# Gate tiles by seven quarter products, with half of the weight sums made by accumulating DMAs

## The chip, the core and the metric

The kernel runs on one core of a Trainium2 chip. TensorE (PE) does matrix products into PSUM, VectorE (DVE) and ScalarE (ACT) do elementwise work, GpSimd (POOL) does little here, and SyncE (SP) issues the DMAs. The metric is the device time of one execution in microseconds. The kernel before takes 1191.26 us (median of 3 runs, 1188.45 to 1191.48).

## The reference, cut to what matters

A decoder of two layers on 512 tokens of width 1024: layer 0 mixes with a gated DeltaNet, layer 1 with sliding-window attention, and after the mixer each layer has a feed-forward part. All is float32. The change lies in the feed-forward part alone:

```python
def swiglu(h, w_gate_up, w_down):
    gu = h @ w_gate_up
    return (jax.nn.silu(gu[..., :D_FF]) * gu[..., D_FF:]) @ w_down
...
    x = x + swiglu(rms_norm(x, ln_ffn[layer]), w_gate_up[layer], w_down[layer])
```

D_FF is 2816, that is 22 tiles of 128 columns for the gate and 22 for the up half.

## The kernel before

Activations lie transposed: 128 features on the partitions, 512 tokens along the free axis, eight such tiles for the width of 1024. A float32 product is made from three matmuls of a rounded type (fp32r): each operand is split into a high half, which is a rounded copy made by ACT (`copy`, line 137), and a low half, which is the rest, made by DVE (`tt`, line 150). `split` (line 165) does both, `weight` (line 179) does it for a weight tile loaded from HBM, into the tags `whi` and `wlo` of the weight pool, with three buffers each. `mm3` (line 190) issues the three matmuls: high x high, high x low, low x high. Every matmul of the profile has line 143.

`ffn` (line 829) works on the 22 pairs of gate and up tiles in two halves of 11. In each half the first gate and up tile are plain projections: 8 blocks of 128 rows times 3 matmuls of 512 columns (`project`, line 198). The other ten tiles go two at a time. Both gate tiles of a pair are plain projections into the banks `pj`, scaled by `rstd` on DVE and put through Silu on ACT (`gate`, line 836). The two up tiles of a pair are made together by `up_pair` (line 934): the two weight tiles and the tokens are seen as a 2 x 2 matrix of quarters (512 of the 1024 rows, one of the two tiles; 256 of the 512 tokens), and their product needs seven products of quarters in place of eight (Strassen in Winograd's form). Each of the seven is 4 x 3 = 12 matmuls of 256 columns. They use three PSUM banks `pa`, `pb`, `pc` of the tag `g`; partial results are held by ACT (`held`, tile `fs`), and products 4, 6 and 7 go on adding into `pa`, so each of them may start only when the value before has been read out of it.

The sums of tokens that the seven products want (`t1` to `t4`) are made once per layer by `token_sums` (line 915), four calls, each with five operations on DVE and one split, into tiles `T`. The sums of weights are made for every pair on DVE (lines 943, 944, 946, 947), in two tiles `ws`, and split. So a pair of up tiles uses four slots of split weights: w0 (the first tile), w1 (two sums), w2 (two sums), w3 (half of the second tile). Two more are used by the gate tiles. `put` (line 846) splits the finished activation. After the 11 tiles of a half the down projection follows: 8 chains of 33 matmuls of 512 columns, in the banks `pj`.

The order of instructions on each engine is not that of the program: a planner in the framework puts them in order, with estimated costs, and gives each tile the buffer that it waits for. What an engine has in its queue is then run strictly in that order. SP's DMA queue likewise: a load waits until its buffer is free, and all later loads wait behind it.

Of the kernel before, what the change touches and what calls it, by code (L numbers as in the profile page):

```python
# [9 lines left out]
F32 = mybir.dt.float32  # L10
F32R = mybir.dt.float32r
# [74 lines left out]
class Builder:  # L86
# [139 lines left out]
    def build(self):  # L226
        tc, nc, a = self.tc, self.nc, self.a
        with ExitStack() as st:
            opened = lambda name, **kw: tc.tile_pool(name=name, bufs=1, reuse_waits="tile", **kw)
            pool = lambda name, **kw: st.enter_context(opened(name, **kw))  # L230
            cp = pool("const")
            self.wpool, self.apool = pool("w"), pool("acta")
            self.dpool = pool("scratch", space=DRAM)
            self.load_constants(cp)
            self.weng = nc.vector
            with opened("layer0", side="right") as self.mpool:
                with self.banks(pj=3, g=2, sc=3):
                    with opened("early", side="right") as ep:
                        self.mem_and_norm(ep)
                        self.gates(ep)  # L240
                    with opened("gdn", side="right") as gp:
                        mix = self.gdn(gp)
                    self.bpool, xp = pool("actb"), pool("x")
                    self.x = [self.t(xp, [P, T], F32, f"x{k}") for k in range(KD)]
                    for k in range(KD):
                        nc.sync.dma_start(self.x[k], a["xT"][:, k, :])
                    self.rstd, self.cosT, self.sinT = (self.t(xp, [P, T], F32, n) for n in ("rstd", "cosT", "sinT"))
                    h = self.output(xp, 0, mix, self.bpool)
            with opened("ffn0", side="right") as fp, self.banks(pj=4, g=4):
                self.ffn(fp, xp, 0, h, self.apool, rope=True)  # L250
            with self.banks(pj=2, g=1, qk=1, pt=2, sc=1):
                with opened("swa", side="right") as sp:
                    mix = self.swa(sp)
                h = self.output(xp, 1, mix, self.apool)
            with opened("ffn1", side="right") as fp, self.banks(pj=4, g=4):
                self.ffn(fp, xp, 1, h, self.bpool)

    def load_constants(self, cp):
# [570 lines left out]
    def ffn(self, fp, xp, layer, h, apool, rope=False):  # L829
# [3 lines left out]
        half = FT // 2  # L833
        acts, sums = [], []

        def gate(f):
            ps = self.project(a["wgu"][layer, 2 * f], h, "pj")
            if f == 0:
                self.rstd_from(acc)
                self.use(SILU_SIN)  # L840
            g = self.t(fp, [P, T], F32, "fg", 2)
            self.tt(nc.vector, g, ps, self.rstd, ALU.mult)
            self.fn(g, g, AF.Silu)
            return g

        def put(u):
# [9 lines left out]
        for f0 in (0, half):  # L856
            acts.clear()
            g = gate(f0)
            u = self.t(fp, [P, T], F32, "fu", 3)
            self.tt(nc.vector, u, self.project(a["wgu"][layer, 2 * f0 + 1], h, "g"), g, ALU.mult)  # L860
            put(u)
            for f in range(f0 + 1, f0 + half, 2):
                g = []
                for i in range(2):
                    if f == 1:
                        for _ in range(2 - i):
                            sums.append(self.token_sums(fp, layer, len(sums), h))
                    g.append(gate(f + i))
                if f == 1:
                    sums.append(self.token_sums(fp, layer, len(sums), h))  # L870
                for u in self.up_pair(fp, [a["wgu"][layer, 2 * (f + i) + 1] for i in range(2)], sums, g):
                    put(u)
            self.acc = None
            tail = KD - 2 if f0 and layer else KD
            down = lambda m, j, n, **kw: self.weight(a["wdn"][layer, m][:, (f0 + j) * P:(f0 + j + n) * P], **kw)
            for m in range(tail):
                ps = self.bank("pj")
                for j, n in ((0, 6), (6, 5)):
                    w = down(m, j, n)
                    for k in range(n):  # L880
                        self.mm3(ps, w, k, acts[j + k], j + k == 0, j + k == half - 1)
                add(self.x[m], ps)
                if f0:
                    self.acc = self.accumulate(xp, self.acc, self.x[m], m)
                if rope and f0 == 0 and m == 0:
                    self.rope_tables(fp)
        if tail < KD:
# [9 lines left out]
            for t in parts:  # L897
                acc = self.acc[:, t]
                for m in range(tail, KD):
                    ps = self.bank("pj")[:, t]  # L900
                    for k in range(half):
                        self.mm3(ps, w[m][k // 6], k % 6, [x[:, t] for x in acts[k]], k == 0, k == half - 1)
                    x = self.x[m][:, t]
                    add(x, ps, t)
                    sq = self.t(fp, [P, T], F32, "fg", 2)[:, t]
                    self.square(sq, x)
                    if m < KD - 1:
                        nxt = self.t(xp, [P, T], F32, "sqa", 2)[:, t]
                        self.tt(nc.vector, nxt, acc, sq, ALU.add)
                        acc = nxt  # L910
# [3 lines left out]

    def token_sums(self, fp, layer, j, h):

        q = T // 2
        g0, g1 = (self.gain(G_FFN[layer], j + i) for i in (0, 4))
        x0, x1 = self.x[j], self.x[j + 4]
        c = self.t(fp, [P, q], F32, "fc", 2)  # L920
        raw = self.t(fp, [P, D], F32, "ws", 2)
        t = [raw[:, i * q:(i + 1) * q] for i in range(4)]
        self.ts(c, x0[:, q:], g0, ALU.mult)
        self.stt(t[0], x0[:, :q], g0, c, ALU.mult, ALU.subtract)
        self.stt(t[1], x1[:, q:], g1, t[0], ALU.mult, ALU.add)
        self.stt(t[2], x1[:, q:], g1, c, ALU.mult, ALU.subtract)
        self.stt(t[3], x1[:, :q], g1, t[1], ALU.mult, ALU.subtract)
        hl = self.weight(None, raw=raw, pool=fp, tags=("T", "T"), bufs=8)
        parts = {f"t{i + 1}": [x[:, i * q:(i + 1) * q] for x in hl] for i in range(4)}
        parts["11"] = [x[:, :q] for x in h[j]]  # L930
        parts["21"], parts["22"] = ([x[:, i * q:(i + 1) * q] for x in h[j + 4]] for i in range(2))
        return parts

    def up_pair(self, fp, src, sums, g):

        nc = self.nc
        q = T // 2
        a1 = self.load(src[0])
        a2 = self.load(src[1], fp, 1)
        a11, a12, a21, a22 = a1[:, :T], a1[:, T:], a2[:, :T], a2[:, T:]  # L940
        w0 = self.weight(None, raw=a1)
        s12, s34 = (self.t(fp, [P, D], F32, "ws", 2) for _ in range(2))
        self.stt(s12[:, :T], a21, -1.0, a22, ALU.mult, ALU.subtract)
        self.stt(s12[:, T:], s12[:, :T], -1.0, a11, ALU.mult, ALU.subtract)
        w1 = self.weight(None, raw=s12)
        self.tt(nc.vector, s34[:, T:], a12, s12[:, T:], ALU.subtract)
        self.tt(nc.vector, s34[:, :T], a11, a21, ALU.subtract)
        w2 = self.weight(None, raw=s34)
        w3 = self.weight(None, raw=a22)
        pa, pb, pc = (self.bank("g")[:, :q] for _ in range(3))  # L950

        def product(ps, w, i, b, first):
# [6 lines left out]
            self.copy(o, ps)  # L959
            return o  # L960

        u = [self.t(fp, [P, T], F32, "fu", 3) for _ in range(2)]
        product(pa, w0, 0, "11", True)
        p1 = held(pa)
        product(pb, w0, 1, "21", True)
        self.tt(nc.vector, u[0][:, :q], pb, p1, ALU.add)
        product(pc, w1, 0, "t1", True)
        p5 = held(pc)
        product(pa, w1, 1, "t2", False)
        u2 = held(pa)  # L970
        product(pc, w2, 1, "22", False)
        self.tt(nc.vector, u[0][:, q:], pc, u2, ALU.add)
        self.tt(nc.vector, u[0], u[0], g[0], ALU.mult)
        product(pa, w2, 0, "t3", False)
        self.tt(nc.vector, u[1][:, q:], pa, p5, ALU.add)
        self.tt(nc.vector, u[1][:, q:], u[1][:, q:], g[1][:, q:], ALU.mult)
        product(pa, w3, 0, "t4", False)
        self.tt(nc.vector, u[1][:, :q], pa, g[1][:, :q], ALU.mult)
        return u

    def rstd_from(self, acc, t=slice(0, T)):
# [16 lines left out]
    def rope_tables(self, pool):  # L998

        nc, a = self.nc, self.a  # L1000
        pi = self.t(pool, [P, T], I32, "rpi")
        nc.sync.dma_start(pi, a["positions"].partition_broadcast(P))
        r = self.t(pool, [P, D], F32, "ws", 2)[:, :T]
        n = self.t(pool, [P, T], F32, "fu", 3)
        nc.vector.tensor_copy(r, pi)
        self.ts(r, r, self.consts[:, C_INV:C_INV + 1], ALU.mult)
# [4 lines left out]
            for part in _pieces(turn, 7, 5):  # L1011
                self.stt(r, n, -part, r, ALU.mult, ALU.add)
        self.ts(r, r, math.pi * (1 - 1e-7), ALU.min, -math.pi * (1 - 1e-7), ALU.max)
        sn = self.t(pool, [P, D], F32, "ws", 2)[:, :T]
        self.fn(sn, r, AF.Sin)
        self.ts(self.sinT, sn, self.consts[:, C_SIGN:C_SIGN + 1], ALU.mult)

# [87 lines left out]
    def final(self, fp, squares, t):  # L1105
# [2 lines left out]
        ps = self.bank("g")[:, t]  # L1108
        for k, sq in enumerate(squares):
            self.mm(ps, self.ones, sq, k == 0, k == len(squares) - 1)  # L1110
        two = self.t(fp, [P, D], F32, "ws", 2)
        l, r = (two[:, i * T:(i + 1) * T][:, t] for i in range(2))
        self.fn(l, ps, AF.Ln, scale=1.0 / D, bias=self.eps)
        self.fn(ps, l, AF.Exp, scale=-0.5)
        self.fn(r, l, AF.Exp, scale=-0.5)
# [76 lines left out]
```

## Time and profile before

| | |
|---|---|
| median of 3 runs | 1191.26 us |
| the profiled execution's own time | 1188.53 us |
| its span (first to last instruction) | 1186.8 us |
| PE busy | 1164.9 us (98%) |
| weight loads on PE (overlap the matmuls) | 982.7 us (83%) |
| DVE busy | 766.6 us (65%) |
| ACT busy | 566.7 us (48%) |
| DMA, all loads on SP's queue | 121.19 MB, 32.9% of 16 engines |
| granted TensorE clock | 0.998 of full |

Matmuls are pipelined: a busy time of one is longer than the distance between two starts, so a rate is read from starts. A row of a view in order of time has start, length, engine, line, operation, output <- inputs, shape, and in brackets how long the engine had been idle before it and what ended that. The name of an engine followed by q is its queue.

### The profile page before, as it was taken

The page shows a single profiled execution, that of the slowest core. Times are in us where ns is not written, and L with a number is a line of the kernel's source. Part 1 is how long each engine was busy: PE and PEld are TensorE (multiplying, and loading weights), DVE is VectorE, ACT ScalarE, POOL GpSimd, SP SyncE. Part 2 cuts the span into 40 slices and gives each one's busy share as a digit, 9 for nine tenths or more (in the row PEclk, how much of TensorE's full clock was granted, in tenths as well). Part 3 has the DMA queues.
Part 4 walks back from the last instruction along what each step waited for, and adds up shares of the span by engine and source line. Part 5 has one row for each costly group of instructions (what it writes and reads, how often), then busy time and mean ns, then how long its engine had stood idle before and what let it go on. Part 6 is the DMA issues. An engine that isn't in the chain of part 4 may idle for free.

```text
span 1186.8 us, 17191 instructions
## 1 busy us (share of the span) xinstructions
PE 1164.9 (98%) x6762; PEld 982.7 (83%) x6762; DVE 766.6 (65%) x1338; ACT 566.7 (48%) x1046; POOL 16.8 (1%) x17
## 2 busy tenths in 40 slices
PE   7999999999999999999999999999999999999997
PEld 6888777877889888889888877678899888899886
DVE  5654977767875766456755767769666544657554
ACT  7578662466544432234443547775444322444423
POOL 0210000000000000000000000000000000000000
PEclk9999999999999999999999999999999999999999
DMA  8434352324422333332323421113223334323232
GB/s 301 133 99 119 105 125 90 96 81 161 133 90 89 103 92 98 118 89 90 102 80 94 133 74 35 54 55 108 88 89 111 91 95 117 90 84 120 74 94 87
DMA packets 51045, 121.19 MB, mean 102 GB/s; under 512 B 14300, under 2 KB 17012, under 8 KB 50964
## 3 DMA queue, kind: packets, MB, share of 16 engines
q1 hardware_dynamic: 50964, 120.10, 32.9%
q8 instruction: 53, 0.87, 0.3%
q14 instruction: 28, 0.23, 0.1%
HBM read 113.12 MB, written 6.96 MB: 101 GB/s over the span
## 4 chain that ended last, share of the span: by engine, by line
PE 92%; DVE 4%; ACT 2%; DMA 1%; issue 0%; SPq 0%; DVEq 0%; ACTq 0%
PE pj L143 61%; PE g L143 23%; PE sc L143 6%; PE pt L147 1%; DVE wlo L150 1%; PE g L147 1%; ACT sm L131 1%; DMA wraw<-in_wmk 1%; ACT whi L137 0%; DVE sm L739 0%; PE qk L143 0%; DVE q L150 0%; DVE btmp L150 0%; DVE mx L743 0%; DVE big L150 0%
## 5 line engine op out<-in xcount | busy, mean ns | idle before, releaser
L143 PE MATMUL pj<-h,whi 128*128 128x512 f32 (+1 forms) x964 | 378.4, 393 | 0.2
L143 PE MATMUL pj<-l,whi 128*128 128x512 f32 (+1 forms) x964 | 377.7, 392 | 0.0
L143 PE MATMUL pj<-h,wlo 128*128 128x512 f32 (+1 forms) x964 | 377.3, 392 | 0.0
L137 ACT ACTIVATE whi<-wraw 128x1024 fp32r<-128x1024 f32 (+2 forms) x211 | 197.3, 936 | 330.8 <-PE pj L143 198.0
L150 DVE TENSOR_TENSOR wlo<-wraw,whi 128x1024 fp32r<-128x1024 f32 (+2 forms) x211 | 225.8, 1070 | 138.0 <-ACT whi L137 135.3
L143 PEld LDWEIGHTS pj<-h,whi 128*128 128x128 f32 x964 | 181.1, 188 | 39.0 <-issue 2.6
L143 PEld LDWEIGHTS pj<-h,wlo 128*128 128x128 f32 x964 | 181.4, 188 | 37.9 <-issue 1.9
L143 PEld LDWEIGHTS pj<-l,whi 128*128 128x128 f32 x964 | 181.3, 188 | 36.7 <-issue 1.5
L143 PE MATMUL g<-T,whi 128*128 128x256 f32 x640 | 118.8, 285 | 0.2 <-ACT fs L137 0.2
L143 PEld LDWEIGHTS g<-T,whi 128*128 128x128 f32 x640 | 99.3, 189 | 4.7 <-DVE fu L150 1.1
L137 ACT ACTIVATE whi<-ws 128x1024 fp32r<-128x1024 f32 x40 | 42.4, 1060 | 117.5 <-PE pj L143 106.4
L143 PE MATMUL g<-h,whi 128*128 128x256 f32 (+1 forms) x300 | 92.0, 307 | 0.0
L143 PE MATMUL g<-h,wlo 128*128 128x256 f32 (+1 forms) x300 | 91.5, 305 | 0.0
L143 PE MATMUL g<-l,whi 128*128 128x256 f32 (+1 forms) x300 | 91.4, 305 | 0.0
L143 PE MATMUL g<-T,wlo 128*128 128x256 f32 x320 | 90.3, 282 | 0.0
L150 DVE TENSOR_TENSOR fg<-pj,rstd 128x512 f32<-128x512 f32 x44 | 30.3, 689 | 74.4 <-PE pj L143 74.4
L143 PEld LDWEIGHTS g<-T,wlo 128*128 128x128 f32 x320 | 60.3, 189 | 0.0
L143 PEld LDWEIGHTS g<-h,whi 128*128 128x128 f32 x300 | 57.2, 191 | 3.5 <-issue 0.2
L143 PEld LDWEIGHTS g<-l,whi 128*128 128x128 f32 x300 | 57.1, 190 | 3.5 <-issue 0.5
L143 PEld LDWEIGHTS g<-h,wlo 128*128 128x128 f32 x300 | 57.2, 191 | 2.5 <-issue 0.2
L150 DVE TENSOR_TENSOR fu<-pj,rstd 128x512 f32<-128x512 f32 (+1 forms) x34 | 22.4, 660 | 55.9 <-PE pj L143 55.9
L150 DVE TENSOR_TENSOR wlo<-ws,whi 128x1024 fp32r<-128x1024 f32 x40 | 49.0, 1224 | 6.7 <-ACT whi L137 6.3
(339 smaller groups left out, 1522.6 us busy)
## 6 DMA issues: line engine op xcount, KB each, us to landing
wraw<-in_wgu SPq DMA_DIRECT2D x88, 512.0 KB, 3.5
wraw<-in_win SPq DMA_DIRECT2D x26, 512.0 KB, 3.7
wraw<-in_wdn SPq DMA_DIRECT2D x32, 384.0 KB, 3.1
wraw<-in_wdn SPq DMA_DIRECT2D x32, 320.0 KB, 2.9
wraw<-in_wout SPq DMA_DIRECT2D x16, 512.0 KB, 3.6
wraw<-in_wq SPq DMA_DIRECT2D x8, 512.0 KB, 3.5
x<-in_xT SPq DMA_DIRECT2D x4, 512.0 KB, 8.6
wraw<-in_wmv SPq DMA_DIRECT2D x4, 512.0 KB, 9.0
```

What stands on the lines that cost most here:

```text
L131: ins = self.nc.scalar.activation(out, in_, func, **kw).ins
L137: self.copied = self.nc.scalar.activation(out, in_, AF.Copy, **kw).ins
L143: return self.nc.tensor.matmul(out, lhsT, rhs, start=start, stop=stop, skip_group_check=more).ins
L147: return self.nc.tensor.transpose(out, in_, self.ident[:k, :k]).ins
L150: return eng.tensor_tensor(out=out, in0=a, in1=b, op=op).ins
```

## The change

1. In every pair but the first of a layer (f = 1) the two gate tiles are no longer projected one by one: `gates` makes them by the same seven products as the up tiles, scaled by `rstd`. `up_pair` becomes `quarters`, and is called twice for such a pair.
2. The sums of weights are arranged anew. Two of the four are made by the DMA: SP loads a quarter into a tile `ws`, and POOL issues a transfer that adds another quarter to it on the way from HBM (`accum_op=ALU.add`). The other two are made by DVE in place in the first weight tile, after that tile has been split. The second weight tile is no longer loaded whole, only its last half (`last`).
3. The two sums of the DMA share one slot of split weights (w1 and w4), so the four slots of a set are w0, w1 with w4, w2, w3. The signs of some token sums and read-outs change to fit (`minus`).
4. The bank plan of the feed-forward part goes from `pj=4, g=4` to `pj=2, g=6`. Tiles `fg` have four buffers in place of two, `ws` four half-size ones in place of two; `fc` has one in place of two, and the token sums' raw tile becomes a tag of its own with one buffer in place of a share in `ws`.

```diff
-            with opened("ffn0", side="right") as fp, self.banks(pj=4, g=4):
+            with opened("ffn0", side="right") as fp, self.banks(pj=2, g=6):
...
+        def gates(f):
+            g = self.quarters(fp, [col(f + i, 0) for i in range(2)], sums, (self.rstd, self.rstd), "fg", 4)
+            for x in g:
+                self.fn(x, x, AF.Silu)
             return g
...
             for f in range(f0 + 1, f0 + half, 2):
-                g = []
-                for i in range(2):
-                    if f == 1:
+                if f == 1:
+                    g = []
+                    for i in range(2):
                         for _ in range(2 - i):
                             sums.append(self.token_sums(fp, layer, len(sums), h))
-                    g.append(gate(f + i))
-                if f == 1:
+                        g.append(gate(f + i))
                     sums.append(self.token_sums(fp, layer, len(sums), h))
-                for u in self.up_pair(fp, [a["wgu"][layer, 2 * (f + i) + 1] for i in range(2)], sums, g):
+                else:
+                    g = gates(f)
+                for u in self.quarters(fp, [col(f + i, 1) for i in range(2)], sums, g, "fu", 3):
                     put(u)
...
-        c = self.t(fp, [P, q], F32, "fc", 2)
-        raw = self.t(fp, [P, D], F32, "ws", 2)
+        c = self.t(fp, [P, q], F32, "fc")
+        raw = self.t(fp, [P, D], F32, "raw")
...
-    def up_pair(self, fp, src, sums, g):
+    def quarters(self, fp, src, sums, by, tag, bufs):
...
+        (a11, a12), (a21, a22) = ([c[:, :T], c[:, T:]] for c in src)
         a1 = self.load(src[0])
-        a2 = self.load(src[1], fp, 1)
-        a11, a12, a21, a22 = a1[:, :T], a1[:, T:], a2[:, :T], a2[:, T:]
+        s1, s3 = (self.t(fp, [P, T], F32, "ws", 4) for _ in range(2))
+        nc.sync.dma_start(s1, a21)
+        nc.sync.dma_start(s3, a11)
+        nc.gpsimd.dma_start(s1, a22, accum_op=ALU.add)
+        nc.gpsimd.dma_start(s3, a21, accum_op=ALU.add)
+        last = self.t(fp, [P, T], F32, "wraw", 2)
+        nc.sync.dma_start(last, a22)
         w0 = self.weight(None, raw=a1)
-        s12, s34 = (self.t(fp, [P, D], F32, "ws", 2) for _ in range(2))
-        self.stt(s12[:, :T], a21, -1.0, a22, ALU.mult, ALU.subtract)
-        self.stt(s12[:, T:], s12[:, :T], -1.0, a11, ALU.mult, ALU.subtract)
-        w1 = self.weight(None, raw=s12)
-        self.tt(nc.vector, s34[:, T:], a12, s12[:, T:], ALU.subtract)
-        self.tt(nc.vector, s34[:, :T], a11, a21, ALU.subtract)
-        w2 = self.weight(None, raw=s34)
-        w3 = self.weight(None, raw=a22)
+        two = [self.t(self.wpool, [P, D], F32R, t, 3) for t in ("whi", "wlo")]
+        w1, w4 = ([x[:, i * T:(i + 1) * T] for x in two] for i in range(2))
+        self.split(s1, *w1)
+
+        self.tt(nc.vector, a1[:, :T], s1, a1[:, :T], ALU.add)
+        self.tt(nc.vector, a1[:, T:], a1[:, :T], a1[:, T:], ALU.add)
+        w2 = self.weight(None, raw=a1)
+        self.split(s3, *w4)
+        w3 = self.weight(None, raw=last)
...
         product(pc, w1, 0, "t1", True)
         p5 = held(pc)
-        product(pa, w1, 1, "t2", False)
+        product(pa, w2, 0, "t2", False)
         u2 = held(pa)
         product(pc, w2, 1, "22", False)
         self.tt(nc.vector, u[0][:, q:], pc, u2, ALU.add)
-        self.tt(nc.vector, u[0], u[0], g[0], ALU.mult)
-        product(pa, w2, 0, "t3", False)
-        self.tt(nc.vector, u[1][:, q:], pa, p5, ALU.add)
-        self.tt(nc.vector, u[1][:, q:], u[1][:, q:], g[1][:, q:], ALU.mult)
+        self.tt(nc.vector, u[0], u[0], by[0], ALU.mult)
+        product(pa, w4, 0, "t3", False)
+        self.stt(u[1][:, q:], pa, -1.0, p5, ALU.mult, ALU.subtract)
+        self.tt(nc.vector, u[1][:, q:], u[1][:, q:], by[1][:, q:], ALU.mult)
         product(pa, w3, 0, "t4", False)
-        self.tt(nc.vector, u[1][:, :q], pa, g[1][:, :q], ALU.mult)
+        self.stt(u[1][:, :q], pa, -1.0, by[1][:, :q], ALU.mult, ALU.mult)
         return u
...
-        two = self.t(fp, [P, D], F32, "ws", 2)
-        l, r = (two[:, i * T:(i + 1) * T][:, t] for i in range(2))
+        l, r = (self.t(fp, [P, T], F32, "ws", 4)[:, t] for _ in range(2))
```

The products keep their order: 1 and 2 use w0, 3 uses w1, 4 and 5 use w2, 6 uses w4, 7 uses w3.

More of the change, by code (lines that the diff above doesn't have):

```diff
@@ L254, in build @@
                 h = self.output(xp, 1, mix, self.apool)
-            with opened("ffn1", side="right") as fp, self.banks(pj=4, g=4):
+            with opened("ffn1", side="right") as fp, self.banks(pj=2, g=6):
                 self.ffn(fp, xp, 1, h, self.bpool)
@@ L834, in ffn @@
         acts, sums = [], []
+        col = lambda f, up: a["wgu"][layer, 2 * f + up]
         def gate(f):
-            ps = self.project(a["wgu"][layer, 2 * f], h, "pj")
+            ps = self.project(col(f, 0), h, "pj")
             if f == 0:
@@ L840, in gate @@
                 self.use(SILU_SIN)
-            g = self.t(fp, [P, T], F32, "fg", 2)
+            g = self.t(fp, [P, T], F32, "fg", 4)
             self.tt(nc.vector, g, ps, self.rstd, ALU.mult)
             self.fn(g, g, AF.Silu)
+            return g
+        def gates(f):
+            g = self.quarters(fp, [col(f + i, 0) for i in range(2)], sums, (self.rstd, self.rstd), "fg", 4)
+            for x in g:
+                self.fn(x, x, AF.Silu)
             return g
@@ L859, in ffn @@
             u = self.t(fp, [P, T], F32, "fu", 3)
-            self.tt(nc.vector, u, self.project(a["wgu"][layer, 2 * f0 + 1], h, "g"), g, ALU.mult)
+            self.tt(nc.vector, u, self.project(col(f0, 1), h, "g"), g, ALU.mult)
             put(u)
             for f in range(f0 + 1, f0 + half, 2):
-                g = []
-                for i in range(2):
-                    if f == 1:
+                if f == 1:
+                    g = []
+                    for i in range(2):
                         for _ in range(2 - i):
                             sums.append(self.token_sums(fp, layer, len(sums), h))
-                    g.append(gate(f + i))
-                if f == 1:
+                        g.append(gate(f + i))
                     sums.append(self.token_sums(fp, layer, len(sums), h))
-                for u in self.up_pair(fp, [a["wgu"][layer, 2 * (f + i) + 1] for i in range(2)], sums, g):
+                else:
+                    g = gates(f)
+                for u in self.quarters(fp, [col(f + i, 1) for i in range(2)], sums, g, "fu", 3):
                     put(u)
@@ L904, in ffn @@
                     add(x, ps, t)
-                    sq = self.t(fp, [P, T], F32, "fg", 2)[:, t]
+                    sq = self.t(fp, [P, T], F32, "fg", 4)[:, t]
                     self.square(sq, x)
@@ L917, in token_sums @@
         q = T // 2
+        if j == 0:
+            self.minus = self.t(fp, [P, 4], F32, "minus")
+            self.ts(self.minus, self.gains[:, G_FFN[layer] + 4:G_FFN[layer] + 8], -1.0, ALU.mult)
         g0, g1 = (self.gain(G_FFN[layer], j + i) for i in (0, 4))
+        n1 = self.minus[:, j:j + 1]
         x0, x1 = self.x[j], self.x[j + 4]
-        c = self.t(fp, [P, q], F32, "fc", 2)
-        raw = self.t(fp, [P, D], F32, "ws", 2)
+        c = self.t(fp, [P, q], F32, "fc")
+        raw = self.t(fp, [P, D], F32, "raw")
         t = [raw[:, i * q:(i + 1) * q] for i in range(4)]
@@ L924, in token_sums @@
         self.stt(t[0], x0[:, :q], g0, c, ALU.mult, ALU.subtract)
-        self.stt(t[1], x1[:, q:], g1, t[0], ALU.mult, ALU.add)
+        self.stt(t[1], x1[:, q:], n1, t[0], ALU.mult, ALU.subtract)
         self.stt(t[2], x1[:, q:], g1, c, ALU.mult, ALU.subtract)
-        self.stt(t[3], x1[:, :q], g1, t[1], ALU.mult, ALU.subtract)
+        self.stt(t[3], x1[:, :q], n1, t[1], ALU.mult, ALU.subtract)
         hl = self.weight(None, raw=raw, pool=fp, tags=("T", "T"), bufs=8)
@@ L960, in held @@
             return o
-        u = [self.t(fp, [P, T], F32, "fu", 3) for _ in range(2)]
+        u = [self.t(fp, [P, T], F32, tag, bufs) for _ in range(2)]
         product(pa, w0, 0, "11", True)
@@ L1000, in rope_tables @@
         nc, a = self.nc, self.a
-        pi = self.t(pool, [P, T], I32, "rpi")
+        pi = self.t(pool, [P, T], I32, "wraw", 2)
         nc.sync.dma_start(pi, a["positions"].partition_broadcast(P))
-        r = self.t(pool, [P, D], F32, "ws", 2)[:, :T]
+        r = self.t(pool, [P, T], F32, "ws", 4)
         n = self.t(pool, [P, T], F32, "fu", 3)
@@ L1013, in rope_tables @@
         self.ts(r, r, math.pi * (1 - 1e-7), ALU.min, -math.pi * (1 - 1e-7), ALU.max)
-        sn = self.t(pool, [P, D], F32, "ws", 2)[:, :T]
+        sn = self.t(pool, [P, T], F32, "ws", 4)
         self.fn(sn, r, AF.Sin)
```

## The prediction

> **What bounds the kernel now.** I read the page's totals and its chain first, then the chain of waits over one feed-forward half, then the instructions of one pair in order of time, then the durations by form.
>
> ```profile
> span 1186.8 us, 17191 instructions
> PE 1164.9 (98%) x6762; PEld 982.7 (83%) x6762; DVE 766.6 (65%) x1338; ACT 566.7 (48%) x1046; POOL 16.8 (1%) x17
> PE 92%; DVE 4%; ACT 2%; DMA 1%; issue 0%; SPq 0%; DVEq 0%; ACTq 0%
> ```
>
> TensorE (PE) carries 92% of the chain that ended last, so a change in the feed-forward part is worth what it does to PE's stream there. The chain over the first half of layer 0 (start, length, what; x is the number of matmuls):
>
> ```profile
> 325.29 10.88 PE pj L143 x48
> 336.17 8.77 PE g L143 x72
> 344.93 1.62 PE pj L143 x7
> 346.55 1.44 PE g L143 x12
> 347.99 9.34 PE pj L143 x41
> ...
> 420.81 8.59 PE g L143 x72
> 429.39 0.70 PE pj L143 x3
> ```
>
> This is one pair: 48 matmuls for two gate tiles, 72 for six quarter products, then seven matmuls of the next gate tile, then the seventh product (12). A pair lasts 336.17 to 357.33, 21.16 us. Look at the seven pj matmuls: product 7 adds onto bank pa, and may not start before DVE has read product 6 out of pa. The gate tile of the next pair fills that hole. The stretch by engine (length, then busy time of each):
>
> ```profile
> core 0: us, PE busy (x) PEld busy (x) DVE busy (x) ACT busy (x) POOL busy (x), PEclk, DMA share, GB/s
> 357.16:378.32 21.16, 21.16 (x133) 19.10 (x132) 13.99 (x20) 9.10 (x13) 0.00 (x0) 1.00 0.33 100
> ```
>
> PE has no hole in it, DVE is busy 13.99 of 21.16 us, POOL does nothing. The starts on PE, and the instructions on ACT and DVE around the hole:
>
> ```profile
> 325.12 0.39 PE L143 MATMUL pj<-h,whi 128*128 128x512 f32 x1
> 336.00 0.28 PE L143 MATMUL g<-h,whi 128*128 128x256 f32 x1
> 338.88 0.40 PE L143 MATMUL g<-T,whi 128*128 128x256 f32 x2
> 344.65 0.28 PE L143 MATMUL g<-T,wlo 128*128 128x256 f32 x1
> 344.77 0.40 PE L143 MATMUL pj<-h,whi 128*128 128x512 f32 x1
> ```
>
> ```profile
> 339.01 0.63 ACT L137 ACTIVATE whi<-wraw 128x512 fp32r<-128x512 f32 x1 [0.98 <-PE g L143]
> 339.15 0.42 DVE L150 TENSOR_TENSOR fu<-g,fs 128x256 f32<-128x256 f32 x1 [0.85 <-PE g L143]
> 341.86 1.06 ACT L137 ACTIVATE whi<-wraw 128x1024 fp32r<-128x1024 f32 x1 [0.97 <-PE g L143]
> 344.85 1.06 ACT L137 ACTIVATE whi<-wraw 128x1024 fp32r<-128x1024 f32 x1 [1.66 <-PE g L143]
> 345.02 0.69 DVE L150 TENSOR_TENSOR fu<-fu,fg 128x512 f32<-128x512 f32 x1
> 345.63 0.42 DVE L150 TENSOR_TENSOR fu<-g,fs 128x256 f32<-128x256 f32 x1
> 345.96 1.22 DVE L150 TENSOR_TENSOR wlo<-wraw,whi 128x1024 fp32r<-128x1024 f32 x1
> ```
>
> These lines carry the forecast. There are three slots of split weights (tags whi and wlo, 3 buffers), and ACT refills one the moment PE lets it go: the copy at 339.01 follows the end of product 2 (338.88), the one at 344.85 the end of product 6 (344.65 + 0.12 = 344.77). From that release to the end of the low half (345.96 + 1.22 = 347.18) pass **2.41 us**. It does not hurt now, because the weights that come so late are those of the second gate tile, which starts after 17 of the 41 matmuls from 347.99, at 351.8.
>
> **What the change removes from PE.** A 512-column matmul starts every 10.88/48 = 0.2267 us (325.12 to 336.00), a 256-column one every 8.59/72 = 0.1193. Two gate tiles cost 10.88 us, seven quarter products 84 x 0.1193 = 10.02: 0.86 us less. With the small waits that most pairs show (8.77 + 1.44 = 10.21) it is 0.67. Pairs changed: f = 3, 5, 7, 9 in a layer's first half, all five in the second, so 9 per layer, 18 in all: **15.5 us off** (12.1 at the low end).
>
> [...]
>
> **What it adds on DVE and ACT.**
>
> ```profile
> L150 DVE TENSOR_TENSOR wlo<-wraw,whi 128x1024 fp32r<-128x1024 f32 x12 | 14.7, 1223 | 10.4 <-ACT whi L137 10.3
> L150 DVE TENSOR_TENSOR wlo<-wraw,whi 128x512 fp32r<-128x512 f32 x4 | 2.8, 694 | 0.4
> L150 DVE TENSOR_TENSOR ws<-wraw,ws 128x512 f32<-128x512 f32 x4 | 2.7, 684 | 0.0
> L150 DVE TENSOR_TENSOR fu<-fu,fg 128x512 f32<-128x512 f32 x4 | 2.7, 686 | 0.0
> L150 DVE TENSOR_TENSOR fu<-g,fs 128x256 f32<-128x256 f32 x12 | 5.0, 421 | 3.2 <-PE g L143 3.2
> L153 DVE SCALAR_TENSOR_TENSOR ws<-x,gains,fc x16: 476/480/489, 311.9 to 825.9; 128x256 f32<-128x256 f32 x16
> L137 ACT ACTIVATE whi<-wraw 128x1024 fp32r<-128x1024 f32 x12 | 12.7, 1062 | 16.6 <-PE g L143 16.6
> L137 ACT ACTIVATE whi<-wraw 128x512 fp32r<-128x512 f32 x4 | 2.5, 633 | 3.9 <-PE g L143 3.9
> L137 ACT ACTIVATE fs<-g 128x256 f32<-128x256 f32 x12 | 4.5, 378 | 3.5 <-PE g L143 3.5
> ```
>
> One set of seven products after the change: on DVE two low halves of 1024 (2.45), three of 512 (2.08), two sums (1.37), and the reads of the banks 3 x 0.42 + 0.69 + 2 x 0.48 = 2.91; together 8.81 us in 13 instructions. A pair has two sets and two splits of activations (1.37): 19.0 us in 28 instructions. Neighbours overlap by some 0.08 (345.02 to 345.63 is 0.61 for a 0.69 instruction), so DVE is held about 16.8 us of PE's 20.04, where it now is at 13.99. Not the bound, but a queue in which a late instruction waits. ACT per pair: 2 x (2.12 + 1.90 + 1.13) + 4 x 0.63 = 12.8 us; enough room.
>
> **What it adds to the path.** A set fills four slots' worth of tiles (w0; w1 and w4 in one; w2; w3) and there are three. w3 already takes w0's slot (339.01). The next set's w0 must take a slot that this set's w2 or w1/w4 holds, and those are let go after product 5 and product 6. Now a whole gate tile stands between two sets; after the change the next set follows at once. The order of the program comes from a planner, and the trace cannot say which slot it gives, so both:
> - *w0 takes the slot freed by product 6.* PE then has nothing until DVE has read product 6: by 339.15 against 338.88 the read starts 0.27 late, takes 0.42 to 0.48, and with some 0.2 more to the next matmul PE idles 0.9 us. Where DVE is behind, as in the pair shown, it is the 1.62 us that the seven matmuls fill now (1.55 from start to start). Product 7 (1.43) covers the rest of the 2.41.
> - *w0 takes the slot freed by product 5.* It is ready 2.41 - 1.43 = 0.98 us after product 6. Two matmuls of product 1 and two of product 2 need only the high half, 0.48 us: PE idles 0.50, and more if DVE does a 0.69 us read first, or if w2 or w3 then finds its slot late.
>
> So 0.50 to 1.55 us a boundary; I take the middle, **1.03**, since DVE is fuller than now. Boundaries between sets: 8 in a layer's first half (9 sets), 9 in the second (10 sets), 34 in all: 35.0 us (17.0 to 52.7). At the four ends of halves the down weights (now covered by the x3 row) meet the same rule: 0.5 each (0 to 1), 2.0.
>
> **DMA.**
>
> ```profile
> q1 hardware_dynamic: 50964, 120.10, 32.9%
> wraw<-in_wgu SPq DMA_DIRECT2D x88, 512.0 KB, 3.5
> wraw<-in_wdn SPq DMA_DIRECT2D x32, 320.0 KB, 2.9
> x<-in_xT SPq DMA_DIRECT2D x4, 512.0 KB, 8.6
> ```
>
> Per set SP issues one load of 512 KB and three of 256 KB, POOL two accumulating ones of 256 KB: 1.75 MB in some 11 us, 160 GB/s, where 32.9% of the engines now carries 102. The trace has no accumulating transfer. Bounds: as an ordinary load (2.9), or the slowest load row (8.6); nearest is the 512 KB load, 3.5, as it must read both operands. The sum tile has four buffers, two per set, so it is refilled two sets, some 20 us, ahead; 2.9 + 8.6 fits below that. Cost nothing; the price without cover is a rival below.
>
> **Smaller edits.** The token sums now run one at a time (fc and raw in one buffer): at most 5 x 0.48 + 1.06 + 1.22 = 4.7 us each, 19 in a row. DVE began them at 311.9 and product 3 wants the first at 338.88: 27 us of cover, so nothing; without it some 5 us a layer. pj with two banks instead of four: a down chain of 33 matmuls lasts 33 x 0.2267 = 7.5 us, its read by DVE 0.69, so nothing.
>
> **Sum.** -15.5 + 35.0 + 2.0 = +21.5 us. The profiled execution took 1188.53 (span 1186.8 and 1.7 around it), which is 2.7 under the runs' median 1191.26 and at their lower end. 1188.5 + 21.5 = **1210**. Extremes: -15.5 + 17.0 = +1.5 (1190), and -12.1 + 52.7 + 4 = +44.6 (1233).
>
> **Rivals.**
> 1. *The holes stay covered.* The planner puts work into them, as it does now with seven matmuls. For it: it filled every one so far. Against: what fills them is a gate tile whose weights sat in a slot early, and that tile is gone. At 0.25 us a boundary: 8.5 - 15.5 = -7.0, 1181; at nothing 1173. It decides below 0.46 us a boundary (15.5/34). Chance 0.13.
> 2. *Break-even*: 0.35 to 0.56 us a boundary ((15.5 -/+ 3.6)/34), which needs the slot of product 5, the four high-half matmuls in the hole and DVE in time at nearly every boundary: 1185 to 1192. Against: DVE held 84% of PE's time. Chance 0.08.
> 3. *The accumulating transfers are late.* At 8.6 us each and one after the other, two take 17.2 us where a set takes 10.0 + 1.0: 6.2 us short in each of 38 sets, 235 us, some 1420. It decides from 5.5 us each. Against: 16 engines at a third. Chance 0.05. The Trainium skill, "SBUF — State Buffer", section "Who interferes with whom", says that VectorE in a two-port mode locks GpSimd out, and so starves transfers issued from it; by its list the tensor-tensor work of a set is not of that kind. No run here shows it yet.
>
> The likeliest, 0.74: the slots open a hole at each boundary, 1192 to 1233. The range that leaves out two in ten reaches into rival 1: 1180 to 1230. A measurement tells about 0.3% (3.6 us) from no change. Faster 0.13, same 0.08, slower 0.79.
>
> **What would show it.** In the changed kernel's stretches: a pair of sets 22 us long with PE busy near 20; after product 6 a hole of about 1 us in which PE waits for DVE, wlo or fu/fg; ACT's whi copies waiting on PE g. A quarter product every 0.119 us. POOL's transfers landing well ahead of ACT's copy of s1. I am wrong if PE stays without holes through a half, or if whi waits for DMA.

## The result, and the profile after

The changed kernel takes **1217.36 us** (median of 4 runs, 1215.29 to 1218.59) against 1189.86 for the kernel before in the same runs: ratio 1.0229, 95% interval 1.0206 to 1.0252. It is slower by 27.5 us. The profiled execution took 1217.50 us.

The page's first lines, and its chain by engine and by line:

```profile
span 1215.7 us, 19269 instructions
PE 1164.1 (96%) x7410; PEld 1003.6 (83%) x7410; DVE 818.1 (67%) x1482; ACT 616.0 (51%) x1174; POOL 83.2 (7%) x93
PE 82%; DVE 10%; ACT 3%; issue 3%; DMA 1%; SPq 0%; DVEq 0%; ACTq 0%
PE pj L143 42%; PE g L143 32%; PE sc L143 6%; DVE wlo L150 5%; PE pt L147 1%; ACT fs L137 1%; PE g L147 1%; DVE fu L150 1%; DVE fg L150 1%; ACT sm L131 1%; DMA wraw<-in_wmk 1%; DVE btmp L150 1%; ACT whi L137 0%; DVE big L150 0%; DMA big<-basein 0%
```

PE's share of the chain fell from 92 to 82%; DVE's rose from 4 to 10, half of it the low halves of weights (wlo, 5%). The chain of waits over one set of seven products (start, length, what; rows under 0.05 us are in part left out):

```profile
359.69 5.54 PE g L143 x44
365.23 0.02 issue
365.25 0.39 ACT fs L137
365.65 0.04 issue
365.69 2.89 PE g L143 x22
...
368.67 0.44 DVE fu L150
...
369.17 0.57 issue
369.74 1.23 DVE wlo L150
370.97 0.04 issue
371.01 5.51 PE g L143 x44
```

A set lasts 359.69 to 371.01, 11.32 us, where 84 x 0.1193 would be 10.02. It is the same in nearly every set: the chain leaves PE twice, once over DVE's wlo, once over ACT's fs. The instructions around the first hole, on ACT and DVE, then on PE:

```profile
368.48 1.06 ACT L137 ACTIVATE whi<-wraw 128x1024 fp32r<-128x1024 f32 x1 [0.80 <-PE g L143]
368.67 0.42 DVE L150 TENSOR_TENSOR fu<-g,fs 128x256 f32<-128x256 f32 x1 [2.33 <-PE g L143]
369.13 0.69 DVE L150 TENSOR_TENSOR fu<-fu,fg 128x512 f32<-128x512 f32 x1
369.74 1.22 DVE L150 TENSOR_TENSOR wlo<-wraw,whi 128x1024 fp32r<-128x1024 f32 x1
...
372.74 0.69 DVE L150 TENSOR_TENSOR wraw<-ws,wraw 128x512 f32<-128x512 f32 x1
...
373.68 0.68 DVE L150 TENSOR_TENSOR wraw<-wraw 128x512 f32<-128x512 f32 x1
...
374.72 1.57 ACT L137 ACTIVATE whi<-wraw 128x1024 fp32r<-128x1024 f32 x2
```

```profile
368.28 0.28 PE L143 MATMUL g<-h,wlo 128*128 128x256 f32 x1
368.40 0.41 PE L143 MATMUL g<-T,whi 128*128 128x256 f32 x2
...
369.83 0.28 PE L143 MATMUL g<-h,whi 128*128 128x256 f32 x1
369.95 0.28 PE L143 MATMUL g<-l,whi 128*128 128x256 f32 x1
370.06 0.28 PE L143 MATMUL g<-h,whi 128*128 128x256 f32 x1
370.18 0.28 PE L143 MATMUL g<-l,whi 128*128 128x256 f32 x1
371.01 0.38 PE L143 MATMUL g<-h,wlo 128*128 128x256 f32 x1 [0.55 <-DVE wlo L150]
```

Product 5 ends at 368.40, and ACT copies the next set's w0 at 368.48: the planner gave it the slot freed by product 5. Product 6 (on T) follows, then the four matmuls that want the high half alone, then PE stands from 370.30 (0.12 after the last start, 370.18) until 371.01, 0.71 us, for the low half.

The second hole follows from the first. w2's sums overwrite the tile that w0 is split from, so they can run only after that split, which ends at 370.96. DVE runs four other instructions before it makes them (372.74 and 373.68), w2 is copied at 374.72, and at product 4 of the next set PE waits again. In the set before, the same wait is 365.29 to 365.69, 0.40 us:

```profile
364.51 1.83 DVE L150 TENSOR_TENSOR wlo<-wraw,whi 128x1024 fp32r<-128x1024 f32 x2 [0.19 <-ACT whi L137]
...
365.25 0.38 ACT L137 ACTIVATE fs<-g 128x256 f32<-128x256 f32 x1 [0.26 <-PE g L143]
...
365.69 0.39 PE L143 MATMUL g<-h,whi 128*128 128x256 f32 x1 [0.24 <-ACT fs L137]
...
365.91 0.28 PE L143 MATMUL g<-T,wlo 128*128 128x256 f32 x1
```

The profile puts this wait down to ACT's `fs`, and that needs a word. Product 4 has run its first two matmuls, which need w2's high half only. The next one needs w2's low half, which comes at about 365.73 (the first of the two instructions from 364.51, at 1.22 us). The planner has put one matmul of product 5 ahead of it (`h,whi`), and that one adds into `pc`, so it waits until ACT has read product 3 out of `pc`, at 365.63. The two releases lie 0.1 us apart: by these figures PE would still have stood for the low half, had ACT been early. In e1 and e2, below, product 4 runs through without that matmul in its midst and without a wait.

Where the 27.5 us are: the stretches between the feed-forward halves agree to within 0.3 us in the two chains (from the end of a half to the first tile of the next, 70.73 and 70.51 us in layer 0). The four halves took 106.31, 106.31, 106.90 and 106.28 us before and 112.86, 113.39, 112.82 and 113.39 after: 26.7 us more. The profiled execution also reached the first half 2.6 us later (327.85 against 325.29). The edit doesn't touch what runs before, the traces of the six experiments reach this point between 326.5 and 330.5 us, and single executions of either kernel lie about 3 us apart, so this part is not put down to the change.

### The profile page after: what moved, and what is told of

It is laid out like the page before. It is cut to its first block, busy times and chain, and to the rows that moved or that the text cites. A ratio compares the mean times of both kernels' runs of the same rounds, so it can differ in the third digit from the quotient of the medians.

```text
span 1215.7 us, 19269 instructions
## 1 busy us (share of the span) xinstructions
PE 1164.1 (96%) x7410; PEld 1003.6 (83%) x7410; DVE 818.1 (67%) x1482; ACT 616.0 (51%) x1174; POOL 83.2 (7%) x93
## 4 chain that ended last, share of the span: by engine, by line
PE 82%; DVE 10%; ACT 3%; issue 3%; DMA 1%; SPq 0%; DVEq 0%; ACTq 0%
PE pj L143 42%; PE g L143 32%; PE sc L143 6%; DVE wlo L150 5%; PE pt L147 1%; ACT fs L137 1%; PE g L147 1%; DVE fu L150 1%; DVE fg L150 1%; ACT sm L131 1%; DMA wraw<-in_wmk 1%; DVE btmp L150 1%; ACT whi L137 0%; DVE big L150 0%; DMA big<-basein 0%
## 5 line engine op out<-in xcount | busy, mean ns | idle before, releaser
L137 ACT ACTIVATE whi<-wraw 128x1024 fp32r<-128x1024 f32 (+3 forms) x249 | 225.6, 921 | 254.2 <-PE pj L143 173.4
L150 DVE TENSOR_TENSOR wlo<-wraw,whi 128x1024 fp32r<-128x1024 f32 (+3 forms) x249 | 259.6, 1054 | 96.3 <-ACT whi L137 95.4
L143 PE MATMUL pj<-h,whi 128*128 128x512 f32 (+1 forms) x676 | 266.1, 395 | 0.2
L143 PE MATMUL pj<-h,wlo 128*128 128x512 f32 (+1 forms) x676 | 265.1, 392 | 1.1 <-DVE wlo L150 1.1
L143 PE MATMUL pj<-l,whi 128*128 128x512 f32 (+1 forms) x676 | 265.5, 393 | 0.0
L143 PE MATMUL g<-T,whi 128*128 128x256 f32 x1216 | 222.8, 281 | 0.0
L143 PEld LDWEIGHTS g<-T,whi 128*128 128x128 f32 x1216 | 187.3, 189 | 0.4
L143 PE MATMUL g<-T,wlo 128*128 128x256 f32 x608 | 171.7, 282 | 0.7 <-DVE wlo L150 0.7
L143 PE MATMUL g<-h,whi 128*128 128x256 f32 (+1 forms) x516 | 154.5, 302 | 7.6 <-ACT fs L137 7.6
L143 PE MATMUL g<-l,whi 128*128 128x256 f32 (+1 forms) x516 | 150.4, 294 | 0.0
```

The costliest lines, as they stand in the source:

```text
L137: self.copied = self.nc.scalar.activation(out, in_, AF.Copy, **kw).ins
L143: return self.nc.tensor.matmul(out, lhsT, rhs, start=start, stop=stop, skip_group_check=more).ins
L150: return eng.tensor_tensor(out=out, in0=a, in1=b, op=op).ins
```

## The experiments

All are compared with the kernel before on the same chip. Each has the time first, then the range of its runs, then the ratio with its 95% interval. Beside the slots theory, that the holes are there because a set's four weight tiles share three slots, stand two others: that DVE serves its fuller queue too late whatever the slots (DVE theory), and that the sums made by the DMA come late (accumulation theory).

### e1: w3 in tiles of its own

```diff
-        w3 = self.weight(None, raw=last)
+        w3 = [self.t(fp, [P, T], F32R, "w3" + x) for x in "hl"]
+        self.split(last, *w3)
...
-            g = self.t(fp, [P, T], F32, "fg", 4)
+            g = self.t(fp, [P, T], F32, "fg", 2)
...
```

> Edit: the changed kernel, with w3 split into two half-size tiles of its own instead of a slot of the weight pool (room from fg, two buffers instead of four). A set then fills three slots (w0; w1 with w4; w2) of three, and the next w0 takes the slot that product 2 lets go. Slots theory (the hole at each boundary is there because four tiles share three slots): the holes of a set (11.30 us against 84 x 0.1193 = 10.02) go, a set lasts 10.0 to 10.2 us, 34 x 1.2 = 41 us less than 1217: 1177 (1172 to 1184), so faster than before as well. DVE theory (DVE, busy 8.47 of 11.30 us in a set, serves its queue too late whatever the slots): a set stays at 11 us or more, 1205 to 1217. Accumulation theory (the sums of the DMA, 6.3 us to land, come late): no difference, 1217.

**1175.48 us** (1173.47 to 1176.74), ratio 0.9878 (0.9863 to 0.9893): faster than the changed kernel by 41.9 us, and than the kernel before by 1.2%. A stretch of 80 us inside a half, by engine (length, then busy times), after and in e1:

```profile
520.00:600.00 80.00, 73.90 (x591) 70.83 (x589) 59.55 (x99) 41.93 (x73) 12.16 (x14) 1.00 0.65 158
```

```profile
520.00:600.00 80.00, 80.00 (x664) 79.35 (x663) 66.64 (x109) 48.51 (x79) 10.38 (x12) 1.00 0.61 153
```

PE's holes are gone: 664 matmuls in 80 us in place of 591, 0.1205 us each, 10.12 a set. DVE is busier than in the changed kernel (66.64 against 59.55 us), and it is in time. One copy of w3 and the next copy of w0 on ACT:

```profile
521.84 0.63 ACT L137 ACTIVATE w3h<-wraw 128x512 fp32r<-128x512 f32 x1 [1.04 <-PE g L143]
...
523.75 1.06 ACT L137 ACTIVATE whi<-wraw 128x1024 fp32r<-128x1024 f32 x1 [0.40 <-ACT h L137]
```

In this stretch product 3 begins at 523.62; the slot that product 2 let go then is filled with the next w0 at 523.75, and that is first used at 529.33, after products 3 to 6. The DVE and accumulation theories, which had 1205 or more, fall here. The smaller number of buffers for fg has no run of its own; with it alone the planner puts every engine's instructions in the same order as in the changed kernel, so it isn't what let w0 in earlier.

### e2: w4 in tiles of its own

```diff
-        w1, w4 = ([x[:, i * T:(i + 1) * T] for x in two] for i in range(2))
+        w1 = [x[:, :T] for x in two]
+        w4 = [self.t(fp, [P, T], F32R, "w4" + x) for x in "hl"]
```

> Edit: the changed kernel, with w4 in two half-size tiles of its own, so that the tile of w1 is let go after product 3 instead of product 6; w3 still takes a slot of the pool (fg with two buffers for the room). Slots theory: w0 of the next set takes the slot freed by product 3, so the first hole of a set (0.71 us, PE waiting for wlo after four matmuls) goes; w2 still has to wait for a slot freed by product 7, or by product 2 of its own set, so the second hole (0.40 us, at product 4) stays or grows: 1217 - 34 x 0.71 = 1193 (1185 to 1200). DVE theory and accumulation theory: 1217.

**1178.24 us** (1175.49 to 1183.45), ratio 0.9908 (0.9878 to 0.9938). Better than I expected: the second hole went too.

```profile
520.00:600.00 80.00, 80.00 (x661) 79.07 (x660) 66.54 (x111) 49.13 (x81) 10.41 (x12) 1.00 0.63 156
```

The same three slots hold here four tiles, as in the changed kernel; only the tile of w1 is let go after product 3 and no longer after product 6. So it isn't the number of tiles alone, but how long the shared one is held. And the second hole was no wait for a slot, as I had put it, but a follow-on of the first: with w0 split early, its tile is free for w2's sums early. The copies of the next w0 and w2 on ACT:

```profile
526.61 1.06 ACT L137 ACTIVATE whi<-wraw 128x1024 fp32r<-128x1024 f32 x1 [0.75 <-ACT whi L137]
...
533.98 1.06 ACT L137 ACTIVATE whi<-wraw 128x1024 fp32r<-128x1024 f32 x1 [0.99 <-PE g L143]
```

w0 comes after product 3, 4.4 us before its first use (530.97). w2 is copied as soon as product 7 lets its slot go (533.84), with products 2 and 3, 2.9 us, still ahead of its use; in the changed kernel product 7 ended at 373.01, and the copy came 1.7 us later, for want of the sums, which were done at 374.36.

### e3: the new sums, with gate tiles as before

```diff
+                g = []
+                for i in range(2):
+                    if f == 1:
...
+                    g.append(gate(f + i))
...
-                else:
-                    g = gates(f)
```

> Edit: one part of the change alone. Up tiles by the new arrangement (two sums by the accumulating DMA, two on DVE in place, w1 and w4 in one slot, six banks g), gate tiles by plain projections as before. Slots theory: a gate tile stands between two sets again and fills the holes, though the slot for it comes after product 5: within 4 us of before, 1186 to 1194, a pair of 21.1 to 21.3 us. DVE theory: the same, since DVE has less to do than before. Accumulation theory: the up sets wait for the sums of the DMA, a pair well above 21.3 us, 1200 or more.

**1202.63 us** (1201.71 to 1203.11), ratio 1.0105 (1.0088 to 1.0122): a miss. Without a single gate tile made by quarters the new arrangement of the sums costs 13 us. The chain of e3 over one pair, and ACT's copy at its hole:

```profile
359.86 7.17 PE g L143 x60
...
367.12 0.44 DVE fu L150
...
367.62 0.57 issue
368.19 1.23 DVE wlo L150
...
369.47 0.73 PE pj L143 x2
370.20 1.42 PE g L143 x12
371.62 10.00 PE pj L143 x44
```

```profile
366.93 1.06 ACT L137 ACTIVATE whi<-wraw 128x1024 fp32r<-128x1024 f32 x1 [0.93 <-PE g L143]
```

It is the hole of the changed kernel, and the late wlo at 368.19 is that of the next *gate* tile. I had counted on the gate tile to fill the hole, and overlooked that it needs a slot too: in the kernel before it gets the one of product 4 (copy at 341.86, 2.9 us before the hole), here that of product 5 (366.93). A pair takes 21.76 us (359.86 to 381.62) in place of 21.16; over 20 pairs that is 12 of the 13 us. So the first hole does not need gate tiles made by quarters, and with e2 the cause is w1 and w4 in one slot, which only product 6 lets go.

### e4: gate tiles by quarters, the old sums

```diff
+                    g = self.up_pair(fp, [a["wgu"][layer, 2 * (f + i)] for i in range(2)], sums, (self.rstd, self.rstd), "fg", 2)
+                    for x in g:
+                        self.fn(x, x, AF.Silu)
+                for u in self.up_pair(fp, [a["wgu"][layer, 2 * (f + i) + 1] for i in range(2)], sums, g, "fu", 3):
...
-            with opened("ffn1", side="right") as fp, self.banks(pj=4, g=4):
+            with opened("ffn1", side="right") as fp, self.banks(pj=2, g=6):
```

> Edit: the other part alone. Gate tiles by seven products too, but all four sums of weights on DVE as before, each pair of sums a slot (w0, w1, w2, w3), no accumulating DMA; banks pj 2, g 6. Slots theory: slots are let go after products 2, 4, 6 and 7; w3 takes the first and w0 of the next set the one of product 4, 4.3 us ahead of its use, so no hole at the start of a set; but DVE has 21.1 us of work in a pair of 20.04 (19 with the overlap of neighbours) and becomes tight: 1180 to 1205. DVE theory: clearly slower than the changed kernel, 1225 or more. Accumulation theory: the waits for the DMA sums are gone, 1175 to 1185.

**1225.05 us** (1220.78 to 1228.91), ratio 1.0295 (1.0267 to 1.0323): outside the range of the slots theory, and as the DVE theory had it. But the chain of e4 over some 40 us, by line and then at one place, named something else:

```profile
by line: PE g L143 30.7%; DMA wraw<-in_wgu 28.3%; DVE wlo L150 8.9%; DVE fu L150 8.3%; DVE ws L153 8.2%; DVE ws L150 4.5%; ACT whi L137 3.8%; issue 3.1%; DVE l L150 3.0%; ACT fg L131 1.6%; ACT fs L137 0.9%; DVE fg L150 0.9%; DVEq L150 0.1%;
...
369.56 3.68 DMA wraw<-in_wgu
373.24 0.02 issue
373.26 0.69 DVE ws L153
```

The sums on DVE wait for a load of 3.7 us. The second weight tile has one buffer in `up_pair`; as long as two gate tiles stood between two sets, its load had 11 us of cover, and now it starts (369.56) when DVE has read the last of the one before (369.54). That is another buffer that the faster order runs out of, so e6 gives it a second.

### e5: e3 with w3 in tiles of its own

The edit is that of e1, made on e3 (the buffers of fg included).

> Edit: e3 (new arrangement of the sums, gate tiles plain) with w3 in two half-size tiles of its own, as in e1. Slots theory, with e3's surprise explained by it (the gate tile after a set needs a slot too, and gets the one of product 5, 1.43 us before it is due, where before it got the one of product 4): the slot of product 2 now serves the gate tile, the hole after product 6 is filled again, a pair is back at 21.1 us, 1188 to 1192. If the accumulating DMA or its traffic costs by itself: stays near e3, 1198 or more.

**1190.13 us** (median of 10, 1187.93 to 1192.28), ratio 1.0006 (0.9996 to 1.0016): no different from the kernel before. The explanation of e3 holds, and two accumulating transfers a pair cost nothing that shows at this precision.

### e6: e4 with a second buffer for that load

```diff
-        a2 = self.load(src[1], fp, 1)
+        a2 = self.load(src[1], fp, 2)
```

> Edit: e4 (gate tiles by seven products, all four sums on DVE) with two buffers in place of one for the second weight tile. Load theory (in e4 the sums wait for a load of 3.6 us that can start only when DVE has let go the single buffer; the chain of e4 has 28% of it): the load is early, and what is left is DVE's amount of work, 19 of 20.04 us a pair: 1178 to 1195. DVE theory (DVE's amount of work and its order set e4's time): little changes, 1212 to 1225, with PE still waiting for wlo, whi and fs.

**1176.73 us** (1175.62 to 1178.62), ratio 0.9893 (0.9873 to 0.9912): 48 us faster than e4 by one buffer, and level with e1. The same stretch as above:

```profile
520.00:600.00 80.00, 80.00 (x664) 79.16 (x663) 72.83 (x116) 46.72 (x73) 0.00 (x0) 1.00 0.30 89
```

DVE is busy 72.83 of 80 us, 91%, PE has no hole, POOL does nothing. The DVE theory falls for e4 too. Moving two sums to the DMA takes 6.2 us of 80 off DVE (66.64 in e1 against 72.83) and nothing that shows off the time: the runs of e1 and e6 overlap.

## Why the prediction was right

**Direction and mechanism.** Forecast 1210 (1180 to 1230, slower 0.79), measured 1217.36. The hole at each boundary is there, where it was put, and e1 and e2 take it away by the slots.

**What was luck.** The 1.03 us was the middle of two cases. The case that came true was priced at 0.50, and by that alone the sum is 1192, no change that could be told. What lifted it were two additions that the prediction names there and does not add up (a read by DVE ahead of the low half, and a late w2); together they came to 0.6 us. So the mechanism was right, and the nearness of the number is in part luck.

**The gain on PE.** Forecast 0.86 us a pair, 15.5 in all. With the holes gone a pair is 2 x 10.12 = 20.24 us against 21.16, 0.92 less, 16.6 in 18 pairs; of this e1 kept 14.0 (1189.49 to 1175.48) and e6 12.8.

**The boundary, the term that was too small.** Forecast 1.03 us (0.50 to 1.55). A set takes 11.30 to 11.32 us, 1.28 to 1.30 over 10.02 and 1.18 over the 10.12 of e1, which has no hole: the two holes of 0.71 and 0.40, and 0.07 that these rows don't separate. The second of the two cases was the true one, the slot of product 5 and four matmuls on the high half. To its 0.50 came 0.2 because DVE did two reads first (368.67 and 369.13 are ahead of wlo; ACT's copy was done at 369.54, wlo began at 369.74). The rest is the second hole, for which I had named the slot and which was the chain w0, its sums, w2.

**The sum.** Forecast -15.5 + 35.0 + 2.0 = 21.5 us. With the gain of 16.6 and 34 x 1.18 = 40.1 for the boundaries it is 23.5; the halves show 26.7. The 3.2 between them are the four ends of halves, forecast 2.0, and what these rows don't separate.

**DVE and ACT.** DVE held 16.8 us a pair by forecast; two sets of the changed kernel (359.69 to 382.31) have 7.91 and 9.03, 16.9. That DVE would be a queue and not the bound is what e6 shows at 91%.

**Token sums, banks.** Costed at nothing. In the pair f = 1, where the token sums are first wanted, PE runs 48 and 60 matmuls without a hole (327.85 to 345.90), and the stretches outside the halves did not grow.

**The rivals.** The holes did not stay covered. The late accumulating transfers fell with e1 and e5, though one transfer takes longer than the 5.5 us from which I said that it would decide (6.3). That price was for two one after the other, and here they are in flight together: POOL starts the two issues 0.66 us apart (365.23 and 365.89), and they land after 5.9 and 7.0 us (medians of their lines, 957 and 958). I also reasoned that gate tiles by quarters are what opens the holes, since they take the filler away. e3 has the first hole with the filler in place, and e6 has none without it: it is the sharing of a slot that opens it, and with the old sums and one more buffer the same gate tiles are 1% faster than the kernel before.

## What to carry to other kernels

When a filler between two stages is taken out, count for each rotating buffer when it is let go and how long its refill takes (here 2.4 to 2.6 us from the last matmul to the usable low half), not only how busy the engines are: e1, e2 and e6 took 42, 39 and 48 us off with 4 KB per partition, which e1 and e2 took from fg. Two tiles in one buffer are held until the later of the two is done, and that shows in whoever comes next in the rotation, not where the sharing was made. Before work is moved off an engine, it pays to try whether that engine is late at all: DVE at 91% cost nothing that shows here.

## What the hardware showed beside

The accumulating transfers took more of the DMA engines' time per byte than the others. The queues of the changed kernel (packets, MB, share of 16 engines) and its loads of 256 KB (count, size, median us to landing):

```profile
q1 hardware_dynamic: 61908, 130.06, 35.1%
q0 software_dynamic: 10944, 19.93, 10.2%
...
ws<-in_wgu SPq DMA_DIRECT2D x76, 256.0 KB, 2.9
ws<-in_wgu POOLq DMA_DIRECT2D x76, 256.0 KB, 6.3
...
wraw<-in_wgu SPq DMA_DIRECT2D x38, 256.0 KB, 6.0
```

A megabyte took 0.51% on POOL's queue, which carries the accumulating transfers, and 0.27% on SP's, 1.9 times as much; in e1 the same bytes took 10.6 and 35.8%, 1.9 times again. No run has a plain load on POOL's queue, so the addition and the queue are not told apart. The time to landing does not tell them apart either: an accumulating 256 KB landed after 6.3 us and the plain load ahead of it after 2.9, but the plain 256 KB of `last`, issued just behind, took 6.0. The Trainium skill, "Collectives: The Full Stack", section "The bandwidth ceiling: the fold count and why AG ≠ RS ≠ AR", says of a ReduceScatter between ranks that its add needs two source reads and that its rate is about half that of a copy. The 1.9 here is of that size; that it has the same cause is not shown by any run.
